# An encoder layer on one core: stores of a half on another queue, rows read in another order, and a rearranged opening

## The chip, the cores and the metric

The kernel runs on one core of a Trainium2 chip. TensorE multiplies (PE in the profile), VectorE (DVE), ScalarE (ACT) and GpSimd (POOL) do the rest, and SyncE (SP) issues most of the transfers. ScalarE and GpSimd have transfer queues of their own. The metric is the device time of the one launch in microseconds (us); lower is better. The inputs lie in the chip's main memory at the start, and both outputs have to be there at the end.

## The reference, cut to what matters

Two token sequences, `x_sample` (512 tokens) and `x_prompt` (1024 tokens), pass the same layer of width 1024 with the same weights:

```python
def trunk(x):                      # D_MODEL = 1024, D_FF = 4096, all in float32
    xn = rmsnorm(x, norm_mix_g)
    qa, ka, va, qb, kb, vb, ga, gb = split(xn @ w_in)
    o_a = grouped_query_attention(rope(rmsnorm(qa)), rope(rmsnorm(ka)), va)   # 8 heads of 64, 2 kv heads
    o_b = neighbourhood_attention(qb, kb, vb, b_rel_pos_bias)                 # 8 heads, 8x16 window
    merged = sigmoid(ga) * (o_a @ w_proj_a) + sigmoid(gb) * (o_b @ w_proj_b)
    x = x + merged @ w_out
    x = x + relu(rmsnorm(x, norm_mlp_g) @ w_mlp_up) ** 2 @ w_mlp_down
    return rmsnorm(x, norm_final_g)

def rmsnorm(x, g):
    return x * rsqrt(mean(x * x, -1) + 1e-6) * g
```

## The kernel before

**Tiles and products.** Tokens are handled in tiles of 128, in which a token is a partition and the 1024 features lie along the row. For a product the tile is transposed on TensorE (eight products of 128x128 with the identity). Every product is made three times to keep the accuracy of float32: an operand is split into a rounded upper part (names with `h` or `hi`, rounded by a copy on ScalarE) and what is left (`l` or `lo`, a subtraction on VectorE), and `mm3` (L203 to L205) multiplies hi by hi, hi by lo and lo by hi into one bank. So a weight block as it is loaded (`raw...`) passes ScalarE and VectorE before TensorE can use it.

**Stages.** `run` treats the sequences one after the other. The first trunk is `x_sample` (names with `0_` or rows 0 to 511), the second `x_prompt` (names with `1_` or rows 512 to 1535). In each it makes the normalised tiles and the products for q, k and v; then grouped-query attention, in which `ss` is a tile of scores, `ps` its exponentials (ScalarE), `pTs` the transposed exponentials in a bank, `pths` and `ptls` their split parts (ScalarE, VectorE) and `os` the output; then neighbourhood attention; then the output projections. The gate products (`gpss`, evicted by ScalarE into `sgs`) fill the attention's waits, and weights of the next step (`wghs`, `wgls`, `wh_vs`, `wl_vs`) are rounded meanwhile. After both trunks `mlp` makes the up and down products of both sequences together, by blocks.

**The opening.** Only the first trunk has it, as nothing covers its loads there. `ask_row` loads the weights of the first norm as one row (`grow`) and as a column form (`g8`), and sets a row of ones. `first_norm` sends six transposes of the identity into TensorE (`warm_up`), spreads the row over all 128 partitions by two products with `ones` (a product over one row; TensorE's records show each as two), and starts the norm of the first tile. `hi_of` and `lo_of` round the first weight blocks, `p0_first` transposes the first tile and splits it, `amid` is what it does between the two halves of that. `load_pad` and `setup_bias` (L168 to L177) load the relative position bias and write it back shifted into a buffer in main memory (`shifted`).

**The output stage of the second trunk.** `w_out` is applied in two halves of 512 columns (`for half in range(2)`), each over the eight token tiles `tt`. In the second half, for each tile: the old rows are read (`xr`), the product `op` is added, the sum is stored to `hd` (the residual, in main memory), squared on ScalarE and normalised, and the norm is stored to `hnd`. For the tiles 4 to 7 (`later`) the norm is made later, and `xr` has a slot of the tag `k4`, of which there are four, shared with the sums and norms of the tiles before. After tile 2 the norms are read back in pairs of tiles by `hn_raw` (rows `hn0_t`, j and j + 3, in slots of the tag `raw`, of which there are three), and after the tiles 3, 4 and 5 `pair_t` transposes a pair for the up product: `pt` at L331, pairs 0, 1 and 2, sixteen transposes each, the first eight from the tile j and the other eight from the tile j + 3.

**What sets the order.** A scheduler places the instructions of each engine by estimated costs; those under `tc.keep_in_program_order` stay as written in their engine's order. A change in one place can so rearrange others that no edited line names. Each queue of transfers issues in order: a load that waits for its slot holds those behind it.

## Time and profile before

| what | value |
|---|---|
| three runs | 2133.28, 2132.10, 2132.61 us |
| median | 2132.61 us |
| the profiled execution | 2133.53 us |
| its span, first to last instruction | 2131.8 us |
| granted TensorE clock, mean | 1.00 |
| TensorE, weight load | 2112.1 us (99%), 1848.0 us (87%) |
| VectorE, ScalarE, GpSimd | 1472.3 us (69%), 1116.1 us (52%), 390.7 us (18%) |
| moved | 264.85 MB read, 87.88 MB written, 165 GB/s |

The span is that of one profiled execution, 1.7 us shorter than the time of the same execution, which is 0.92 us above the median. A share is busy time over the span. In the rows of the timeline the first number is the start of the work in us from the span's start and the second its length; what stands in square brackets is the idle time of the engine just before and what ended it.

### The profile page before, as it was taken

The page shows a single profiled execution, that of the slowest core. Times are in us where ns is not written, and L with a number is a line of the kernel's source. Part 1 is how long each engine was busy: PE and PEld are TensorE (multiplying, and loading weights), DVE is VectorE, ACT ScalarE, POOL GpSimd, SP SyncE. Part 2 cuts the span into 40 slices and gives each one's busy share as a digit, 9 for nine tenths or more (in the row PEclk, how much of TensorE's full clock was granted, in tenths as well). Part 3 has the DMA queues.
Part 4 walks back from the last instruction along what each step waited for, and adds up shares of the span by engine and source line. Part 5 has one row for each costly group of instructions (what it writes and reads, how often), then busy time and mean ns, then how long its engine had stood idle before and what let it go on. Part 6 is the DMA issues. An engine that isn't in the chain of part 4 may idle for free.

```text
span 2131.8 us, 31800 instructions
## 1 busy us (share of the span) xinstructions
PE 2112.1 (99%) x10967; PEld 1848.0 (87%) x10967; DVE 1472.3 (69%) x2810; ACT 1116.1 (52%) x2351; POOL 390.7 (18%) x508
## 2 busy tenths in 40 slices
PE   9999999999999999999999999999999999999998
PEld 8887788988898888888888899999999988888887
DVE  6674686777667754657772877778777777659663
ACT  5664564566546644555431566566655643433352
POOL 3332420433233323433301200003000000000000
PEclk9999999999999999999999999999999999999999
DMA  6445567521221132433472666578444799688561
GB/s 188 136 124 147 155 192 244 187 72 35 58 86 54 40 112 84 126 101 110 145 244 101 206 200 193 161 248 210 158 145 158 259 356 336 214 269 286 177 198 69
DMA packets 319595, 350.92 MB, mean 165 GB/s; under 512 B 31168, under 2 KB 255048, under 8 KB 319433
## 3 DMA queue, kind: packets, MB, share of 16 engines
q1 hardware_dynamic: 278071, 279.91, 41.8%
q10 hardware_dynamic: 35682, 51.93, 7.0%
q0 software_dynamic: 5680, 17.04, 2.8%
q8 instruction: 87, 1.43, 0.3%
q14 instruction: 75, 0.61, 0.1%
HBM read 264.85 MB, written 87.88 MB: 165 GB/s over the span
## 4 chain that ended last, share of the span: by engine, by line
PE 82%; DVE 3%; DMA 2%; issue 2%; ACT 2%; POOL 1%; SPq 1%; ACTq 0%; POOLq 0%; DVEq 0%
PE dn L203 7%; PE dn L205 7%; PE dn L204 7%; PE pTs L827 3%; PE gpss L203 3%; PE gpss L205 3%; PE gpss L204 3%; PE uc L203 2%; PE uc L204 2%; PE ud L204 2%; PE ud L203 2%; PE ud L205 2%; PE uc L205 2%; PE ua L205 2%; PE ua L204 2%; PE ua L203 2%
## 5 line engine op out<-in xcount | busy, mean ns | idle before, releaser
L204 PE MATMUL dn<-wd,ah 128*128 128x512 f32 (+1 forms) x624 | 242.6, 389 | 0.0
L205 PE MATMUL dn<-wd,al 128*128 128x512 f32 (+1 forms) x624 | 242.6, 389 | 0.0
L203 PE MATMUL dn<-wd,ah 128*128 128x512 f32 (+1 forms) x624 | 242.6, 389 | 0.0
L1347 ACT ACTIVATE ah<-ar 128x512 fp32r<-128x512 f32 x168 | 104.2, 627 | 196.3 <-PE dn L204 172.8
L1348 DVE TENSOR_TENSOR al<-ar,ah 128x512 fp32r<-128x512 f32 x168 | 115.7, 696 | 73.2 <-ACT ah L1347 63.9
L205 PEld LDWEIGHTS dn<-wd,al 128*128 128x128 f32 x624 | 117.2, 188 | 24.3
L203 PEld LDWEIGHTS dn<-wd,ah 128*128 128x128 f32 x624 | 117.2, 188 | 24.0
L204 PEld LDWEIGHTS dn<-wd,ah 128*128 128x128 f32 x624 | 117.2, 188 | 24.0
L793 POOL TENSOR_SCALAR ps<-ps,rls 128x1024 f32<-128x1024 f32 (+1 forms) x96 | 96.8, 1010 | 215.7 <-DVE rls L792 205.1
L833 DVE TENSOR_TENSOR ptls<-pTs,pths 128x512 fp32r<-128x512 f32 x160 | 107.8, 687 | 39.2 <-ACT pths L832 38.6
L832 ACT ACTIVATE pths<-pTs 128x512 fp32r<-128x512 f32 x160 | 94.2, 598 | 74.1 <-PE pTs L827 71.4
L787 DVE TENSOR_REDUCE nms<-ss 128x1 f32<-128x1024 f32 (+1 forms) x96 | 99.7, 1041 | 22.3 <-PE ss L785 22.0
L188 POOL TENSOR_TENSOR rs_f<-ms_f,mhalf 128x1 f32<-128x1 f32 x6 | 4.0, 667 | 590.7 <-DVE ms_f L184 590.7
L203 PE MATMUL gpss<-xs_0h,w_gs 128*128 128x512 f32 x256 | 104.8, 409 | 1.5 <-DVE ptls L833 1.3
L790 ACT ACTIVATE ps<-ss,nms 128x1024 f32<-128x1024 f32 (+1 forms) x96 | 93.1, 971 | 23.1 <-DVE nms L787 20.6
L827 PEld LDWEIGHTS pTs<-ident,ps 128*128 128x128 f32 x640 | 78.1, 140 | 28.2 <-POOL ps L793 4.4
L204 PE MATMUL gpss<-xs_0l,w_gs 128*128 128x512 f32 x256 | 101.1, 395 | 0.0
L205 PE MATMUL gpss<-xs_0h,w_gs 128*128 128x512 f32 x256 | 101.0, 395 | 0.0
L827 PE MATMUL pTs<-ident,ps 128*128 128x128 f32 x640 | 98.9, 274 | 1.2 <-DVE ptls L833 0.3
L1347 ACT ACTIVATE A<-S 128x512 fp32r<-128x512 f32 x128 | 76.1, 624 | 31.9 <-DVE S L1410 26.7
L1348 DVE TENSOR_TENSOR A<-S,A 128x512 fp32r<-128x512 f32 x128 | 84.6, 686 | 4.3 <-ACT A L1347 4.3
L1466 ACT ACTIVATE c<-c 128x384 f32<-128x384 f32 x97 | 50.7, 524 | 69.3 <-DVE c L1465 69.2
(352 smaller groups left out, 6408.3 us busy)
## 6 DMA issues: line engine op xcount, KB each, us to landing
ar<-ud SPq DMA_DIRECT2D x120, 512.0 KB
br<-in_w_mlp_down_dram SPq DMA_DIRECT2D x72, 512.0 KB
rawu<-in_w_mlp_up_dram SPq DMA_DIRECT2D x64, 512.0 KB
ud<-c ACTq DMA_DIRECT2D x128, 192.0 KB
raw_gs<-in_w_in_dram SPq DMA_DIRECT2D x32, 512.0 KB
zgs<-sgs ACTq DMA_DIRECT2D x48, 256.0 KB
ud<-cs SPq DMA_DIRECT2D x64, 192.0 KB
raw_os<-in_w_out_dram SPq DMA_DIRECT2D x16, 512.0 KB
```

What stands on the lines that cost most here:

```text
L203: nc.tensor.matmul(out, ah, bh, start=start, stop=False, **kw)
L204: nc.tensor.matmul(out, ah, bl, start=False, stop=False, **kw)
L205: nc.tensor.matmul(out, al, bh, start=False, stop=stop, **kw)
L787: nc.vector.tensor_reduce(nm_, s, axis=AX.X, op=ALU.max, negate=True)
L790: nc.scalar.activation(p, s, AF.Exp, bias=nm_, accum_out=l)
L793: nc.gpsimd.tensor_scalar(p, p, rl, 1.0, op0=ALU.mult, op1=ALU.mult)
L827: nc.tensor.transpose(pt[:, j * P : (j + 1) * P], PP[u, j][:, kc * P : (kc + 1) * P], ident)
L832: nc.scalar.activation(hi, pt, AF.Copy)
L833: nc.vector.tensor_tensor(lo, pt, hi.bitcast(F32), op=ALU.subtract)
L1347: nc.scalar.activation(hi, src, AF.Copy)
L1348: nc.vector.tensor_tensor(lo, src, hi.bitcast(F32), op=ALU.subtract)
L1466: nc.scalar.activation(t, t, AF.Relu)
```

## The change

It has two groups of edits. In the opening, the norm weights are loaded into row 0 of a whole tile that is set to zero first, and the ones stand in row 0 of a tile of zeros, so that the spreading products contract over 128 rows in place of one; the warm-up has twelve transposes in place of six; and the rounding of the second weight block is cut in a lower and an upper half, of which the upper is rounded between the two halves of the first tile's split, with its subtraction on GpSimd. In the output stage of the second trunk, the sums of the second half's tiles 0 to 3 are stored by ScalarE's queue in place of SyncE's, and the rows `xr` of the tiles 5 to 7 are asked for between the reads of the norms.

```diff
--- before.py
+++ after.py
@@ -117,17 +117,19 @@
         )
 
     def ask_row(src, pool):
-        row = pool.tile([P, D], F32, tag="xn", name="grow", bufs=2)[0:1, :]
-        nc.scalar.dma_start(row, bass.AP(tensor=src.tensor, offset=src.offset, ap=[[0, 1], [1, D]]))
+        row = pool.tile([P, D], F32, tag="xn", name="grow", bufs=2)
+        tc.keep_in_program_order(nc.vector.memset(row, 0.0))
+        nc.scalar.dma_start(row[0:1, :], bass.AP(tensor=src.tensor, offset=src.offset, ap=[[0, 1], [1, D]]))
         g8 = sgp.tile([P, 512], F32, tag="sg", name="g8", bufs=2)[0:NC8, 0:P]
         nc.scalar.dma_start(g8, bass.AP(tensor=src.tensor, offset=src.offset, ap=[[P, NC8], [1, P]]))
-        ones = sgp.tile([P, 512], F32, tag="sg", name="ones", bufs=2)[0:1, 0:P]
-        tc.keep_in_program_order(nc.vector.memset(ones, 1.0))
+        ones = sgp.tile([P, 512], F32, tag="sg", name="ones", bufs=2)[:, 0:P]
+        tc.keep_in_program_order(nc.vector.memset(ones, 0.0))
+        tc.keep_in_program_order(nc.vector.memset(ones[0:1, :], 1.0))
         return row, g8, ones
 
     def first_norm(xt, gb, row, g8, ones, pool, nm):
 
-        warm_up(6)
+        warm_up(12)
         pt = big("grow")
         for q in range(2):
             qs = slice(q * 512, q * 512 + 512)
@@ -561,13 +563,15 @@
                         tc.keep_in_program_order(nc.sync.dma_start(x23[:, i, :], x[(2 + i) * P : (3 + i) * P, :]))
                         xt_of[2 + i] = x23[:, i, :]
 
-                    def hi_of(part, kb):
+                    lower, upper = slice(0, 2), slice(2, 4)
+
+                    def hi_of(part, kb, a=slice(0, 4)):
                         s_, cs = src[part, kb]
-                        tc.keep_in_program_order(nc.scalar.activation(wh[kb][:, :, cs], s_, AF.Copy))
-
-                    def lo_of(part, kb, eng=nc.vector):
+                        tc.keep_in_program_order(nc.scalar.activation(wh[kb][:, a, cs], s_[:, a], AF.Copy))
+
+                    def lo_of(part, kb, eng=nc.vector, parts=(lower, upper)):
                         s_, cs = src[part, kb]
-                        for a in (slice(0, 2), slice(2, 4)):
+                        for a in parts:
                             tc.keep_in_program_order(
                                 eng.tensor_tensor(
                                     wl[kb][:, a, cs], s_[:, a], wh[kb][:, a, cs].bitcast(F32), op=ALU.subtract
@@ -577,11 +581,13 @@
                     hi_of("q", 0)
                     xn, gcol = norm_rest()
                     lo_of("q", 0)
-                    hi_of("q", 1)
+                    hi_of("q", 1, lower)
                     st1 = []
 
                     def amid():
-                        lo_of("q", 1)
+                        hi_of("q", 1, upper)
+                        lo_of("q", 1, parts=(lower,))
+                        lo_of("q", 1, nc.gpsimd, (upper,))
                         st1.append(tr.stat(1, ph, x1, True))
 
                     tr.p0_first(xn, gcol, amid)
@@ -1160,13 +1166,24 @@
             def tmp_zs(name):
                 return ph.tile([P, 512], F32, tag="zs", name=name, bufs=6 if nxt is not None else 8)
 
-            def hn_raw(j):
+            def hn_raw(j, between=None):
                 res = []
                 for t in (j, j + 3):
                     r = rawp.tile([P, 1024], F32, tag="raw", name=f"hn0_{t}")
                     nc.sync.dma_start(r, hnd[t * P : (t + 1) * P, :])
                     res.append(r)
+                    if between:
+                        between.pop(0)()
                 return res
+
+            xr_of = {}
+
+            def rows_late(tt):
+                xr = ph.tile([P, D], F32, tag="k4", name=f"xr{N}_1_{tt}", bufs=4)[:, 0:512]
+                op = nc.sync.dma_start(xr, x[tt * P : (tt + 1) * P, 512:1024])
+                if tt == NT - 1:
+                    tc.keep_in_program_order(op)
+                xr_of[tt] = xr
 
             def pool_wp(shape, dt, name):
                 return ph.tile(shape, dt, tag="k4", name=name, bufs=4)
@@ -1232,10 +1249,12 @@
 
                     later = half == 1 and nxt is None and tb == 1
                     if later:
-                        xr = ph.tile([P, D], F32, tag="k4", name=f"xr{nm}", bufs=4)[:, 0:512]
+                        if tt not in xr_of:
+                            rows_late(tt)
+                        xr = xr_of.pop(tt)
                     else:
                         xr = tmp_zs(f"xr{nm}")
-                    nc.sync.dma_start(xr, x[tt * P : (tt + 1) * P, hc])
+                        nc.sync.dma_start(xr, x[tt * P : (tt + 1) * P, hc])
                     ht = hs_[tt // 2][:, tt % 2, :] if tb == 0 else None
                     if ht is None and half == 1 and not later:
                         ht = ph.tile([P, D], F32, tag="k4", name=f"ht{nm}", bufs=4)
@@ -1279,7 +1298,7 @@
                         if half == 1 and nxt is not None:
                             tc.keep_in_program_order(op)
                         if nxt is None:
-                            (nc.sync if half == 1 else nc.gpsimd).dma_start(hd[rows_, hc], ht[:, hc])
+                            (nc.scalar if half == 1 else nc.gpsimd).dma_start(hd[rows_, hc], ht[:, hc])
                         elif half == 1:
                             st = slice(0, D) if tb == 0 else hc
                             nc.gpsimd.dma_start(hd[rows_, st], ht[:, st])
@@ -1316,7 +1335,8 @@
                                 banks = [b_[:, q * 512 : q * 512 + 512] for b_ in both for q in range(2)]
                                 pair_t(f"0_{j}", j, hn_t, B0, banks, tmp_zs)
                                 if j < 2:
-                                    hn_t = hn_raw(j + 1)
+                                    early = [lambda: [rows_late(t) for t in (5, 6)], lambda: rows_late(7)]
+                                    hn_t = hn_raw(j + 1, early if j else None)
             while ahead:
                 nxt.p0_t(*ahead.pop(0))
```

The rows below are instructions in the order in which an engine has them, with the line, the operation and the program's names with a number for each tile; the line numbers of the kernel after are 2 to 20 higher.

SyncE's queue in the output stage of the second trunk, before; `hd` and `hnd` are the buffers in main memory, `hn0_t` the norms read back, `xrs1_1_t` the old rows of tile t:

```order
L1238 DMA xrs1_1_3_12766<-in_x_prompt_dram 128x512
L1282 DMA hd_86<-hs1_0_12388 128x512 x2
L1282 DMA hd_86<-hs1_1_12389 128x512 x2
L1167 DMA hn0_4_12864<-hnd_87 128x1024
L1238 DMA xrs1_1_4_12866<-in_x_prompt_dram 128x512
L1167 DMA hn0_2_12937<-hnd_87 128x1024
L1238 DMA xrs1_1_5_12941<-in_x_prompt_dram 128x512
L1238 DMA xrs1_1_6_13015<-in_x_prompt_dram 128x512
L1238 DMA xrs1_1_7_13044<-in_x_prompt_dram 128x512
L1167 DMA hn0_5_12939<-hnd_87 128x1024
```

The same place after:

```order
L1257 DMA xrs1_1_3_12775<-in_x_prompt_dram 128x512
L1173 DMA hn0_4_12873<-hnd_87 128x1024
L1183 DMA xrs1_1_4_12875<-in_x_prompt_dram 128x512
L1173 DMA hn0_2_12946<-hnd_87 128x1024
L1183 DMA xrs1_1_5_12948<-in_x_prompt_dram 128x512
L1183 DMA xrs1_1_6_12950<-in_x_prompt_dram 128x512
L1173 DMA hn0_5_12952<-hnd_87 128x1024
L1183 DMA xrs1_1_7_12954<-in_x_prompt_dram 128x512
```

The four stores to `hd` have left the queue, and the last read of a norm (`hn0_5`) stands ahead of the last old rows, not behind them. The stores are now on ScalarE, each ahead of the square of its tile. On TensorE pair 1 of the transposes stands six products later, pair 2 three.

TensorE in the first trunk's attention, before; `waits` is what an instruction waits for by semaphore:

```order
L785 MATMUL ss0_0_3_0_2_1103<-kTs0_0_215,qTs0_0_1_214 128x512
L804 MATMUL os0_0_1_0_1028<-ptls0_0_1_0_3_1037,vhls0_0_216 128x512
L827 MATMUL pTs0_0_2_0_2_1127<-ident_88,ps0_0_2_0_0_950 128x128 [waits Activation_49]
L827 MATMUL pTs0_0_2_0_2_1127<-ident_88,ps0_0_2_0_1_961 128x128
L827 MATMUL pTs0_0_2_0_2_1127<-ident_88,ps0_0_2_0_2_986 128x128
L827 MATMUL pTs0_0_2_0_2_1127<-ident_88,ps0_0_2_0_3_1019 128x128
L203 MATMUL gpss0_2304_3_0_1147<-xs0_0h0_158,w_gs0_2304_3_890 128x512 [waits DVE_49]
L204 MATMUL gpss0_2304_3_0_1147<-xs0_0l0_160,w_gs0_2304_3_890 128x512
L205 MATMUL gpss0_2304_3_0_1147<-xs0_0h0_158,w_gs0_2304_3_890 128x512
L784 MATMUL ss0_0_3_0_3_1136<-kTs0_0_215,qTs0_0_1_214 128x512 [waits Activation_49]
L785 MATMUL ss0_0_3_0_3_1136<-kTs0_0_215,qTs0_0_1_214 128x512
```

The same place after:

```order
L791 MATMUL ss0_0_3_0_2_1112<-kTs0_0_224,qTs0_0_1_223 128x512
L810 MATMUL os0_0_1_0_1037<-ptls0_0_1_0_3_1046,vhls0_0_225 128x512
L790 MATMUL ss0_0_3_0_3_1145<-kTs0_0_224,qTs0_0_1_223 128x512 [waits Activation_49]
L791 MATMUL ss0_0_3_0_3_1145<-kTs0_0_224,qTs0_0_1_223 128x512
L833 MATMUL pTs0_0_2_0_2_1136<-ident_88,ps0_0_2_0_0_959 128x128 [waits DVE_49]
L833 MATMUL pTs0_0_2_0_2_1136<-ident_88,ps0_0_2_0_1_970 128x128
L833 MATMUL pTs0_0_2_0_2_1136<-ident_88,ps0_0_2_0_2_995 128x128
L833 MATMUL pTs0_0_2_0_2_1136<-ident_88,ps0_0_2_0_3_1028 128x128
L205 MATMUL gpss0_2304_3_0_1156<-xs0_0h0_166,w_gs0_2304_3_899 128x512 [waits Activation_49]
```

The score tile `ss0_0_3_0_3` has moved ahead of the four transposes and of the gate product; the transposes now wait for VectorE, and the gate product for ScalarE.

ScalarE at the same place, before; `pths` are the upper parts of transposed exponentials, `sgs` the evicted gate product:

```order
L463 ACTIVATE sgs0_2304_2_0_1117<-gpss0_2304_2_0_891 128x512
L192 ACTIVATE wghs0_1_0_913<-rawkvs0_1_927 128x4x128
L192 ACTIVATE wghs0_1_1_917<-rawkvs0_1_927 128x4x128
L832 ACTIVATE pths0_0_2_0_0_1063<-pTs0_0_2_0_0_1058 128x512
L192 ACTIVATE wh_vs0_1_0_1048<-raw_vs0_1_0_1046 128x1024
L790 ACTIVATE ps0_0_3_0_1_1083,ls0_0_3_0_1_1084<-ss0_0_3_0_1_1078,nms0_0_3_0_1_1081 128x512
L192 ACTIVATE wh_vs0_1_0_1048<-raw_vs0_1_4_1053 128x1024
L832 ACTIVATE pths0_0_2_0_1_1099<-pTs0_0_2_0_1_1094 128x512
```

The same place after:

```order
L194 ACTIVATE wghs0_1_0_922<-rawkvs0_1_936 128x4x128
L194 ACTIVATE wghs0_1_1_926<-rawkvs0_1_936 128x4x128
L194 ACTIVATE wh_vs0_1_0_1057<-raw_vs0_1_0_1055 128x1024
L838 ACTIVATE pths0_0_2_0_0_1072<-pTs0_0_2_0_0_1067 128x512
L796 ACTIVATE ps0_0_3_0_1_1092,ls0_0_3_0_1_1093<-ss0_0_3_0_1_1087,nms0_0_3_0_1_1090 128x512
L194 ACTIVATE wh_vs0_1_0_1057<-raw_vs0_1_4_1062 128x1024
L838 ACTIVATE pths0_0_2_0_1_1108<-pTs0_0_2_0_1_1103 128x512
L465 ACTIVATE sgs0_2304_2_0_1126<-gpss0_2304_2_0_900 128x512
```

The eviction `sgs` has moved from the first place to the last, and the first `wh_vs` ahead of the first `pths`. On VectorE two subtractions of `wl_vs` now stand ahead of the `ptls` of the same transposes.

In the opening the order on ScalarE is: `g8`, then `grow` (before: the other way round), the square of the first tile, the first weight block, half of the second, the first four pieces of the tile's split, the other half, the square of the second tile, the other four pieces. VectorE starts with the zeros of the whole row tile and the two settings of `ones`. On SyncE the load of the bias (`pad`) now leads its part of the queue, ahead of the first values' weights (`raw_vs_0_0`), and the first store to `shifted` stands ahead of the second `raw_vs` and of three loads for the rotary tables.

## The prediction, as recorded before the changed kernel ran

> **What bounds the kernel now.** I read the page first, then the waits of TensorE, then the order of time around each place that the change touches.
>
> ```profile
> span 2131.8 us, 31800 instructions
> PE 2112.1 (99%) x10967; PEld 1848.0 (87%) x10967; DVE 1472.3 (69%) x2810; ACT 1116.1 (52%) x2351; POOL 390.7 (18%) x508
> ```
>
> TensorE is idle for 2131.8 - 2112.1 = 19.7 us in all, so removed waits can bring no more than that; beyond it only a faster TensorE clock can. The change adds six small transposes to TensorE and removes nothing, so its value is idle time moved about. Two of the longest single waits stand where the change acts:
>
> ```profile
> PE pt L331 <- DMA hn<-hnd: 1.5, 1, 1.5
> PE gpss L203 <- DVE ptls L833: 1.3, 1, 1.3
> ```
>
> Columns: who waits for whom, us in total, how often, the longest. The first is in the output projection of the second trunk, the second in the first trunk's attention, which no line of the diff names, but whose order the scheduler has rearranged.
>
> **Term 1: the late stores and reads (1150 to 1200 us).** SyncE's queue, the chain that ended last, TensorE, and the price of a store issued by ScalarE:
>
> ```profile
> 1151.56 16.65 SPq L1282 DMA_DIRECT2D hd<-hs  x4
> 1180.69 0.44 SPq L1167 DMA_DIRECT2D hn<-hnd  x1
> ...
> 1171.56 8.66 DMA hnd<-xnhs
> 1180.69 4.57 DMA hn<-hnd
> ...
> 1175.76 1.91 PE L331 MATMUL pt<-ident,hn 128*128 128x128 f32 x16
> 1182.07 0.39 PE L203 MATMUL ops<-wh_os,mgs 128*128 128x512 f32 x1
> 1182.30 0.39 PE L204 MATMUL ops<-wl_os,mgs 128*128 128x512 f32 x1
> 1182.81 1.06 PE L331 MATMUL pt<-ident,hn 128*128 128x128 f32 x8
> 1185.39 1.06 PE L331 MATMUL pt<-ident,hn 128*128 128x128 f32 x8 [1.52 <-DMA hn<-hnd]
> ...
> L1288 ACTq DMA_DIRECT2D hd<-xrs x4: 321/326/327, 1129.8 to 1146.1; - x4
> ```
>
> The last row read, hn5, was issued at 1180.69, because ahead of it on SyncE's in-order queue stood the last residual read (xr 7), whose slot came free when the store of 1171.56 had landed, 8.66 us later, at 1180.22. The read then took 4.57 us and TensorE stood 1.52 us. In the changed order hn5 stands ahead of xr 7. What holds it then is its own slot: that of hn1, free after the first eight transposes of pair 1. TensorE's order puts pair 1 six products later; one product takes 0.227 us (1182.07 to 1182.30), so pair 1 starts at 1175.76 + 1.36 = 1177.12. Sixteen transposes take some 1.8, so eight are done at 1178.0. Issue at 1178.1 and 4.57 us give a landing at 1182.7. Pair 2 starts three products later, at 1182.81 + 0.68 = 1183.5, and wants hn5 eight transposes on, at 1184.3: 1.6 us to spare, the wait goes. The start of pair 2 itself was 0.28 late (1182.30 to 1182.81 is 0.51, not 0.23); I count 0.08 of it. Gain 1.6 us. Bounds: 1.8 (both gaps gone); and if hn5 took 8.66 us it would land at 1186.8, 2.5 late, a loss of 1.0.
>
> The four stores moved from SyncE to ScalarE cost ScalarE 0.33 us each (L1288's row), and each stands ahead of the square of the same tile, so the norm and its store come 0.33 later; nothing waits for these within 1.6 us. What waits on ScalarE behind a store waits for the same VectorE sum that the square needs anyway. SyncE loses the four stores that held its queue from 1151.56 to 1168.2, so the two reads for pairs 1 and 2 leave about a microsecond sooner; no one waits for those.
>
> **Term 2: the rearranged attention (77 to 88 us).** ScalarE, VectorE and TensorE in order of time:
>
> ```profile
> 77.50 0.60 ACT L463 ACTIVATE sgs<-gpss 128x512 f32<-128x512 f32 x1
> 77.97 1.16 ACT L192 ACTIVATE wghs<-rawkvs 128x512 fp32r<-128x512 f32 x2
> 79.02 0.61 ACT L832 ACTIVATE pths<-pTs 128x512 fp32r<-128x512 f32 x1
> 79.49 1.08 ACT L192 ACTIVATE wh_vs<-raw_vs 128x1024 fp32r<-128x1024 f32 x1
> 80.44 0.71 ACT L790 ACTIVATE ps<-ss,nms 128x512 f32<-128x512 f32 x1
> ...
> 78.66 1.43 DVE L198 TENSOR_TENSOR wgls<-rawkvs,wghs 128x256 fp32r<-128x256 f32 x4 [0.16 <-ACT wghs L192]
> 80.00 0.68 DVE L833 TENSOR_TENSOR ptls<-pTs,pths 128x512 fp32r<-128x512 f32 x1
> 80.61 1.29 DVE L198 TENSOR_TENSOR wl_vs<-raw_vs,wh_vs 128x512 fp32r<-128x512 f32 x2
> ...
> 78.85 0.60 PE L827 MATMUL pTs<-ident,ps 128*128 128x128 f32 x4
> 80.74 0.50 PE L203 MATMUL gpss<-xs_0h,w_gs 128*128 128x512 f32 x1 [1.29 <-DVE ptls L833]
> ```
>
> Before, TensorE transposes at 78.85 into the bank that the gate's eviction (sgs, 77.50) had freed, then waits for ptls (80.00, done 80.68). In the new order the next score tile (ss 3_3) comes first, sgs has moved behind two weight roundings and two pths, and two wl_vs come ahead of ptls. By the rows: without sgs ScalarE runs 0.47 ahead; wghs 77.50, wh_vs 78.55, pths 79.50, the exponential 79.97, done 80.68. The score tile needs that exponential's bank, so TensorE stands from 78.85 to 80.7. VectorE: wgls until 79.7, wl_vs (1.2) until 80.9, ptls done at 81.6: the transposes, now in ptls' bank, start at 81.65 (two products end at 81.2: 0.45 idle) and end at 82.0. The next gate product now waits for sgs; ScalarE's second wh_vs (0.95) and pths (0.47) put it at 82.05 to 82.65, 0.7 idle more. Idle 1.85 + 0.45 + 0.7 = 3.0 against 80.74 - 79.2 = 1.5 before (four transposes issue in 0.35). The order behind it has more gate products in reserve, which I let win back 0.2. Loss 1.3 us. Bounds: 0 (an engine runs ahead of these rows) and 1.9 (nothing won back, and one more transpose waits 0.4 for VectorE). Other pieces reordered there had no wait over 0.3, and I give them nothing.
>
> **Term 3: the opening (0 to 18 us).**
>
> ```profile
> 0.73 0.53 ACTq L121 DMA_DIRECT2D grow<-in_norm_mix_g_dram  x1
> 0.90 0.17 DVE L125 MEMSET ones<- 1x128 f32 x1
> 13.28 1.27 DVE L394 SCALAR_TENSOR_TENSOR xns<-xts,rs_s,grow 128x1024 f32<-128x1024 f32 x1
> ...
> 1.35 1.54 PE L163 MATMUL warm<-ident 128*128 128x128 f32 x6 [1.35 <-POOL ident masks.py:199]
> 2.82 3.78 PE L134 MATMUL grow<-grow,ones 1*128 1x512 f32 x4
> 7.64 1.94 PE L410 MATMUL ptxs<-ident,xns 128*128 128x128 f32 x8 [1.03 <-DVE xns L152]
> 10.34 0.58 PE L205 MATMUL zs<-wghs,xs_0l 128*128 128x256 f32 x1 [0.34 <-DVE xs_0l L416]
> 13.07 0.41 PE L205 MATMUL zs<-wghs,xs_0l 128*128 128x256 f32 x1
> 13.60 0.28 PE L205 MATMUL zs<-wghs,xs_0l 128*128 128x256 f32 x1
> 14.94 1.07 PE L291 MATMUL ptxs<-ident,xns 128*128 128x128 f32 x8
> ...
> 8.76 1.14 ACT L413 ACTIVATE xs_0h<-ptxs,gcol 128x128 fp32r<-128x128 f32 x4 [0.20 <-PE ptxs L410]
> 10.81 1.16 ACT L413 ACTIVATE xs_0h<-ptxs,gcol 128x128 fp32r<-128x128 f32 x4
> 12.24 1.12 DVE L416 SCALAR_TENSOR_TENSOR xs_0l<-ptxs,gcol,xs_0h 128x128 fp32r<-128x128 f32 x4
> 12.41 0.56 POOL L188 TENSOR_TENSOR rs_s<-ms_s,mhalf 128x1 f32<-128x1 f32 x1 [5.20 <-DVE ms_s L184]
> ...
> 10.57 0.50 SPq L172 DMA_DIRECT2D pad<-in_b_rel_pos_bias_dram  x1
> 16.79 0.32 SPq L177 DMA_DIRECT2D shifted<-pad  x1
> ```
>
> TensorE's products last 0.41 until 13.07 and 0.28 from 13.60: until then it runs at about half speed, although it was busy without a break from 1.35 to 6.6 with six full transposes and four one-row products.
>
> The new 128x1024 memset starts where the memset of ones did, at 0.90. No row has its price; it lies between 0.17 (1x128) and 1.27 (the VectorE pass of its shape, L394), and I take 1.1, nearest the latter. The row's load waits for it, so it leaves at 2.0 instead of 0.73. It had landed by 2.82, so within 2.1; now by 4.1. Twelve transposes (1.54 for six) end at 4.3, so TensorE does not see that delay. The products end at 4.3 + 3.78 = 8.1 at the old speed, and the transposes of x, wanted at 7.64, would start 0.7 late; if the clock rises by about 6.9, not late.
>
> With the fast clock the first four transposes end 0.5 sooner (eight took 1.94 here, sixteen 1.91 in term 1), so ScalarE's first xs_0h starts at 8.27 instead of 8.76. The upper half of the second weight block, moved behind it, takes the 0.5 back: its second xs_0h stands at 10.82, was 10.81. VectorE gives up 0.6 of subtractions to GpSimd, which idled 5.2 us there, and can start its second xs_0l when the last xs_0h is done (10.81 + 1.16 = 11.97), at 12.02 instead of 12.24. xns and the transposes at 14.94 follow it: gain 0.2 us, and not the two microseconds that the clock would suggest, because VectorE and ScalarE end last there. Bounds: 0.5 gained (the first step's gain passes through whole); 1.0 lost (clock still slow: 0.7 late, and half a block of rounding now in the chain). I take 0.2 gained.
>
> The Trainium skill (TensorE: Matmul & The Clock Gate, Part 1) says that a free-running window of about 3.4 us of sustained matmul activity lifts the clock from half to full. By that alone the clock should have risen before 8.2 us in this trace, and it did not, so here the trace disagrees unless one-row products count for little. By the page term 3 is 0.2 gained to 0.5 lost, depending on where the window falls; if the row count is not what matters, it is the 1.0 lost.
>
> On SyncE pad's load now leads, and shifted, which waits for it, stands ahead of the second raw_vs and three rope loads: with the same 6.2 us (10.57 to 16.79) these leave some 4 us later. The wide slack ahead of their use, past 20 us, covers it; were it gone, ScalarE's rounding of raw_vs would be late next.
>
> **Sum.** 1.6 + 0.2 - 1.3 = 0.5 us gained. The profiled execution took 2133.53 with a span of 2131.8, so 2131.3 and 2133.0; the median of the runs, 0.92 below that execution, goes from 2132.61 to 2132.1. No difference under about 0.2% (4.3 us) can be told from none, and every bound above, even added up, stays inside it.
>
> **Rivals.**
> (a) The new attention order costs nothing: scheduled orders need not meet these rows again. 1.8 gained, 2130.8. For it: only one wait over 1 us stood there before. Against it: both new waits are on banks whose release I can place.
> (b) The other side: the row's load arrives after the twelve transposes, or the clock is late, and the products push the transposes of x. It decides from about 7.4 us as the end of the products: past it each microsecond costs one. Loss there 1.0, in all 1.6 - 1.0 - 1.3 = 0.7 lost, 2133.3. For it: 3.78 us of products now start 1.5 us later. Against it: twelve full transposes lead.
> (c) hn5 is not sooner on time, since the same bytes are in flight: term 1 is nothing, 1.1 lost, 2133.7.
> (d) The clock falls back in the 3 us of idleness at 79 to 83 us. Rising again took from 10.34 to 13.28 of products in the opening, about 3 us at half speed, 1.5 us lost: with the rest 1.0 lost, 2133.6. Against it: the 1.29 us gap here left products at 0.23 spacing. The same page of the Trainium skill says that an idle window of some 3.4 us halves the clock; the gaps here are broken by products, so it hardly applies.
>
> **Chances.** Forecast 0.48 (its own range 2131.1 to 2133.0), (a) 0.22, (b) 0.14, (c) 0.08, (d) 0.03; something unseen beyond 0.2%: 0.03 faster, 0.02 slower. Faster 0.03, same 0.95, slower 0.02. From (a) with both gains at their best (2130.0) to (c) with some noise (2134.2) leaves under 2 in 10 out.
>
> **What would show it.** Term 1: hn5 issued near 1178 and no wait before pair 2. Term 2: TensorE idle at about 79 to 83 for 3 us in three pieces, ended by an exponential, a ptls and an sgs. Term 3: matmuls at 0.28 before 9 us, second transposes of x near 14.7. The prediction is wrong if TensorE's sum of idle time moves by more than 4 us, or if a stretch outside these three does.

## The result and the profile after

The changed kernel takes 2137.26 us (median of 15 runs, 2135.42 to 2139.62) against 2132.61 (15 runs beside it, 2131.31 to 2135.11): 4.65 us slower, ratio 1.002 with a 95% interval of 1.0013 to 1.0027. Forecast were 2132.1 and a range up to 2134.2. Measured again later, the same pair gave 2137.97 against 2133.20 (ratio 1.0022, 1.0013 to 1.0031). Its profiled execution took 2138.04 us.

The head of the page of the changed kernel, and the longest waits of TensorE (who waits for whom, us in total, how often, the longest):

```profile
span 2136.3 us, 31820 instructions
PE 2114.0 (99%) x10973; PEld 1848.6 (87%) x10973; DVE 1472.0 (69%) x2811; ACT 1116.9 (52%) x2352; POOL 391.3 (18%) x509
...
PE grow L136 <- DMA grow<-in_norm_mix_g_dram: 3.1, 1, 3.1
PE obs L1070 <- DVE bhs L1048: 1.8, 3, 1.1
PE ss L790 <- ACT ps L796: 1.8, 1, 1.8
```

The wait for hn is gone from the list, as forecast. A wait of 3.1 us for the row of norm weights and one of 1.8 us in the attention are new, and the waits before obs (0.7 before) have grown. Where the time went is best read by comparing when the same product starts in both profiles. Groups of TensorE's products, with the first and the last start of a group, of the kernel before:

```profile
L203 PE MATMUL gpss<-xs_0h,w_gs x32: 387/390/502, 45.6 to 89.9; 128*128 128x512 f32 x32
L1007 PE MATMUL sbs<-kBs,qBs x192: 279/341/448, 181.1 to 1042.5; 128*128 128x384 f32 x128, 128*128 128x256 f32 x64
L203 PE MATMUL ops<-wh_os,mgs x192: 388/389/476, 329.4 to 1195.4; 128*128 128x512 f32 x192
```

and of the changed kernel:

```profile
L205 PE MATMUL gpss<-xs_0h,w_gs x32: 387/393/793, 48.5 to 97.2; 128*128 128x512 f32 x32
L1013 PE MATMUL sbs<-kBs,qBs x192: 278/341/449, 186.5 to 1049.1; 128*128 128x384 f32 x128, 128*128 128x256 f32 x64
L205 PE MATMUL ops<-wh_os,mgs x192: 388/389/477, 334.7 to 1200.3; 128*128 128x512 f32 x192
```

The first gate product is 2.9 us late (45.6 to 48.5): the opening. The first sbs is 5.4 late (181.1 to 186.5): the attention, which cost 2.8 by 110 us, less 0.3 won back behind it. The last sbs is 6.6 late (1042.5 to 1049.1), so a further piece was lost in the second trunk. The last ops is 4.9 late: the late stage gave 1.7 back against this profile of before. TensorE's idle time as a whole grew only from 19.7 to 22.3 us, since part of the loss is products that ran more slowly.

**The opening.** Issues of ScalarE's and SyncE's queue, and VectorE and TensorE, in order of time, changed kernel:

```profile
0.73 0.61 ACTq L124 DMA_DIRECT2D g<-in_norm_mix_g_dram  x1
2.04 0.23 ACTq L122 DMA_DIRECT2D grow<-in_norm_mix_g_dram  x1
...
0.73 0.38 SPq L262 DMA_DIRECT2D xts<-in_x_sample_dram  x1
1.17 0.97 SPq L541 DMA_DIRECT2D rawqs<-in_w_in_dram  x2
...
1.10 0.91 DVE L121 MEMSET grow<- 128x1024 f32 x1 [0.16 <-issue]
...
1.35 2.82 PE L165 MATMUL warm<-ident 128*128 128x128 f32 x12 [1.35 <-POOL ident masks.py:199]
7.27 3.56 PE L136 MATMUL grow<-grow,ones 128*128 128x512 f32 x4 [3.10 <-DMA grow<-in_norm_mix_g_dram]
10.91 1.09 PE L412 MATMUL ptxs<-ident,xns 128*128 128x128 f32 x8
```

Setting the tile to zero took 0.91 us, and the row left at 2.04 us, as forecast. But the products that need it began only at 7.27, 5.2 us later. Between 0.73 and 2.14 the loads of xts and of both rawqs, 512 KB each, were issued on SyncE's queue, ahead of these 4 KB; in the kernel before the row left beside the first of them. The trace also keeps the single packets that the transfer engines moved, and they show the row waiting behind these loads: its one packet of 4096 bytes began at 6.37 and took 0.16 us, when 870 of the 1024 packets of the two rawqs had started. The small load g, ahead of the row on ScalarE's queue, was done by 2.41, so it is not what held it. In the kernel before the row's packet began at 1.66.

**The attention.** TensorE in order of time, and the granted clock by stretch (columns: stretch, its length, busy time and count of PE, PEld, DVE, ACT, POOL, then PEclk, DMA share, GB/s):

```profile
81.53 0.40 PE L810 MATMUL os<-ptls,vhls 128*128 128x512 f32 x1
83.72 0.50 PE L790 MATMUL ss<-kTs,qTs 128*128 128x512 f32 x1 [1.79 <-ACT ps L796]
84.05 0.40 PE L791 MATMUL ss<-kTs,qTs 128*128 128x512 f32 x1
84.72 0.66 PE L833 MATMUL pTs<-ident,ps 128*128 128x128 f32 x4 [0.27 <-DVE ptls L839]
85.64 0.79 PE L205 MATMUL gpss<-xs_0h,w_gs 128*128 128x512 f32 x1 [0.26 <-ACT sgs L465]
86.22 0.63 PE L206 MATMUL gpss<-xs_0l,w_gs 128*128 128x512 f32 x1
...
85.50:86.00 0.50, 0.36 (x1) 0.37 (x2) 0.50 (x1) 0.50 (x2) 0.09 (x1) 0.59 1.11 334
86.00:88.00 2.00, 2.00 (x6) 1.52 (x6) 2.00 (x6) 1.44 (x4) 0.44 (x1) 0.50 0.99 286
88.90:89.10 0.20, 0.20 (x2) 0.18 (x1) 0.20 (x1) 0.00 (x0) 0.00 (x0) 0.74 0.99 238
```

The three pieces of idleness that the prediction named are there, ended by an exponential, a ptls and an sgs, in this order. Then products take 0.63 us, not 0.39: the granted clock is 0.50 from 85.59 (0.59 over the half microsecond means 0.09 at full speed) to 89.0, for 3.4 us. The Trainium skill (TensorE: Matmul & The Clock Gate, Part 1) gives such a window of about 3.4 us, free-running, and the trace agrees in length. The Trainium skill names an idle window, in the same part, as what halves the clock. Here the window ahead held products for 1.4 of its 3.4 us, and the clock fell all the same.

### The profile page after: what moved, and what is told of

It is laid out like the page before. It is cut to its first block, busy times and chain, and to the rows that moved or that the text cites. A ratio compares the mean times of both kernels' runs of the same rounds, so it can differ in the third digit from the quotient of the medians.

```text
span 2136.3 us, 31820 instructions
## 1 busy us (share of the span) xinstructions
PE 2114.0 (99%) x10973; PEld 1848.6 (87%) x10973; DVE 1472.0 (69%) x2811; ACT 1116.9 (52%) x2352; POOL 391.3 (18%) x509
## 4 chain that ended last, share of the span: by engine, by line
PE 82%; DVE 2%; ACT 1%; issue 1%; DMA 1%; POOL 1%; SPq 0%; ACTq 0%; POOLq 0%; DVEq 0%
PE dn L205 7%; PE dn L206 7%; PE dn L207 7%; PE pTs L833 3%; PE gpss L205 3%; PE gpss L207 3%; PE gpss L206 2%; PE uc L205 2%; PE ud L206 2%; PE uc L206 2%; PE ud L205 2%; PE uc L207 2%; PE ud L207 2%; PE ua L206 2%; PE ua L205 2%; PE ua L207 2%
## 5 line engine op out<-in xcount | busy, mean ns | idle before, releaser
L1367 ACT ACTIVATE ah<-ar 128x512 fp32r<-128x512 f32 x168 | 104.7, 628 | 207.7 <-PE dn L206 186.5
```

Source lines behind the costliest of these rows:

```text
L1367: nc.scalar.activation(hi, src, AF.Copy)
```

## The experiments

The runs were made on three chips, each beside the kernel before, whose median there was 2133.65, 2133.20 and 2133.91 us. The interval of each ratio is about 0.0009 to both sides, 1.9 us, so sizes below that rest on the profiles, and a profile is one execution. The two do not always agree: open_only has the highest median, but its profiled execution took 2136.77 us, less than that of after_again (2137.46). "Lost" and "won" below compare starts of the same products with those in the profile of before; two further profiles with the opening of before (late_only, before_again) run 0.2 us ahead of that one from the opening on, so 0.2 us is no difference there.

| run | median, us | median less that of before, us | ratio, 95% interval |
|---|---|---|---|
| late_only | 2132.97 | -0.7 | 0.9996 (0.9987 to 1.0005) |
| a_warm6 | 2135.27 | +1.6 | 1.0004 (0.9995 to 1.0013) |
| a_copy12 | 2135.37 | +1.7 | 1.0005 (0.9996 to 1.0014) |
| a_copy6 | 2132.78 | -0.9 | 0.9992 (0.9983 to 1.0001) |
| a_onerow | 2134.98 | +1.8 | 1.0007 (0.9998 to 1.0016) |
| open_only | 2138.54 | +5.3 | 1.0022 (1.0013 to 1.0031) |
| after_again | 2137.97 | +4.8 | 1.0022 (1.0013 to 1.0031) |
| best | 2132.21 | -1.7 | 0.9993 (0.9984 to 1.0002) |

The first four were run on the first of these chips, the next three on the second, best on the third. b_round and before_again are one profiled execution each (2132.64 and 2132.40 us).

**late_only**: the kernel before with the late edits of the change, and none of the opening's.

```
...
-                            (nc.sync if half == 1 else nc.gpsimd).dma_start(hd[rows_, hc], ht[:, hc])
+                            (nc.scalar if half == 1 else nc.gpsimd).dma_start(hd[rows_, hc], ht[:, hc])
...
-                                    hn_t = hn_raw(j + 1)
+                                    early = [lambda: [rows_late(t) for t in (5, 6)], lambda: rows_late(7)]
+                                    hn_t = hn_raw(j + 1, early if j else None)
```

> The kernel before with only the late part of the change (stores of the second half on ScalarE's queue, old rows of tiles 5 to 7 asked for between the reads of the norms). Theory of the three places (opening +2.9 us, attention at 79 to 92 us +2.8, late stage -1.7): the late gain stands by itself, so the median is 1.7 us under before, about 2130.9, TensorE has no wait for hn above 0.3 us between 1150 and 1200 us, and nothing differs ahead of 1150 us. Rival: the gain seen there is only the other side of the late opening (queues that had emptied), so the wait for hn stays near 1.5 us and the median within 0.5 us of before.

The profile has no wait of TensorE above 0.2 us between 1150 and 1200 us, and hn5 was issued at 1179.87, ahead of the last old rows. Against the profile of before that is 1.7 us won, as expected. The median says 0.7. Which of the two is right, before_again tells below. That nothing differs ahead of 1150 us did not hold: between 200 and 400 us this profile loses 1.7 us against that of before, although TensorE has the same order in both. Losses of a microsecond in one profile can come and go without any edit.

**a_warm6**: the changed kernel with before's warm-up.

```
-        warm_up(12)
+        warm_up(6)
```

> The changed kernel with six warm-up transposes as before, in place of twelve; everything else of the change stays. Its order in the attention is then that of before. Theory of the three places: the rearranged order in the attention is the cause of the loss there, so the stretch 77 to 92 us costs what it cost before (one wait of about 1.3 us, clock 1.00 throughout) and the median falls by about 2.8 us against the changed kernel, to about 2134.5; the wait for the row of norm weights in the opening grows by the six transposes' 1.4 us, to about 4.5 us. Rival: the clock fell because the opening ran late and shifted the attention against the clock's windows, not because of the order; then a half-clock piece of about 3.4 us stays near 80 us and the median falls by under 1.2 us.

```profile
PE grow L136 <- DMA grow<-in_norm_mix_g_dram: 4.1, 1, 4.1
...
PE gpss L205 <- DVE ptls L839: 1.3, 1, 1.3
```

The wait for the row is 4.1 us and the attention has its old wait of 1.3 us and nothing more: between 70 and 110 us no product loses anything against before (3.4 us late ahead of it and 3.5 behind). So six small transposes at 3 us, which only shift the scheduler's estimates, are what rearranged the attention at 80 us. The rival is out.

**a_copy12**: the row is loaded at once into a tile that is free until later, and copied.

```
+        row1 = gb[0:1, :]
-        nc.scalar.dma_start(row[0:1, :], ...)
+        nc.scalar.dma_start(row1, ...)
...
+        tc.keep_in_program_order(nc.vector.tensor_scalar(row[0:1, :], row1, 1.0, None, op0=ALU.mult))
```

> The changed kernel, but the row of norm weights is loaded at once into the tile gb, which is free until later, and copied from there by VectorE into row 0 of the zeroed tile; all other engines keep the order of the changed kernel. Theory of the three places: the opening's loss is the row's load, which the setting to zero pushed behind the 512 KB loads; loaded at 0.7 us it lands by 2.9, the copy of one row (about 1 us, from 0.91 for setting the whole tile) ends by 4.1, the products start behind the twelve transposes near 4.2 us, and TensorE does not wait for the row; the first transposes of x start no later than 8 us, and the median is 2.9 us under the changed kernel or lower, 2134.4 or less. Rival: the products over 128 rows and the order of the rounding are what costs; then the opening stays late by more than 1.5 us against before and the median within 1 us of 2137.3.

```profile
2.40 0.68 DVE L129 TENSOR_SCALAR grow<-gbs 1x1024 f32<-1x1024 f32 x1
...
3.97 3.60 PE L138 MATMUL grow<-grow,ones 128*128 128x512 f32 x4
7.66 1.09 PE L414 MATMUL ptxs<-ident,xns 128*128 128x128 f32 x8
```

Issued at 0.73, the row was there by 2.40, within 1.7 us, and the products followed the transposes without a wait. The opening's loss is 0.1 us where it was 2.9, with the products over 128 rows and the rounding order still in: the rival is out. That the 512 KB loads are what holds a row issued later is read from the packets above; moving those loads was not tried. The attention lost 2.6 us again, with a half-clock piece from 82.5.

**a_copy6**: the same with six warm-up transposes.

> The row loaded at once and copied, as in the run beside it, and six warm-up transposes, so that the attention has the order of before. Theory of the three places: both losses are gone and the late gain is left, so 2137.3 - 2.9 - 2.8 = 2131.6 at most, and 2130.9 (before less 1.7) if the opening costs what it did before: 1 to 1.7 us under before. The products wait about 1 us for the copy between the warm-up and about 4 us. Rival: a further cost of the change lies elsewhere (a wait of 1.5 us for a weight load near 1015 us stood in the changed kernel's profile too); then it stays at 2132.6 or above.

Both losses are gone: level with before at 60 us, 0.4 late at 110, and 0.9 under before by the median, a little less than the 1 to 1.7 expected. The wait near 1015 us, the rival's further cost, is gone as well, so it comes with the twelve transposes. The clock was up at 4.9 us, and the opening gained nothing by it.

**a_onerow**: the changed kernel with before's spreading of the norm weights (one row, not zeroed) and twelve transposes.

```
-        row = pool.tile([P, D], F32, tag="xn", name="grow", bufs=2)
-        tc.keep_in_program_order(nc.vector.memset(row, 0.0))
-        nc.scalar.dma_start(row[0:1, :], ...)
+        row = pool.tile([P, D], F32, tag="xn", name="grow", bufs=2)[0:1, :]
+        nc.scalar.dma_start(row, ...)
...
-        ones = sgp.tile([P, 512], ...)[:, 0:P]
...
+        ones = sgp.tile([P, 512], ...)[0:1, 0:P]
...
```

> The changed kernel with the spreading of the norm weights as before (one row, loaded at once, products over one row), with its twelve warm-up transposes, its rounding order and its late part. TensorE, SyncE and GpSimd have exactly the changed kernel's order. Theory of the three places: without the zeroed tile there is no wait for the row, and the opening is 0.3 to 1.0 us over before (products end near 8.0, x's transposes wait for them); the clock rises only after a window of whole products, between 10 and 13.5 us, because one-row products do not count as activity. In the attention the order of the changed kernel costs 1.0 us of idle time, and 1.7 us more when the clock's window of 3.41 us holds nearly all of that idle time. Median about 1.4 us over before (0.3 + 2.8 - 1.7), down to 0 if the clock falls in few executions. Rival: one-row products count, so the clock rises by 8.2 us and the first transposes of x take about 1.1 us, not 1.9.

```profile
4.10 3.78 PE L134 MATMUL grow<-grow,ones 1*128 1x512 f32 x4
7.82 1.97 PE L410 MATMUL ptxs<-ident,xns 128*128 128x128 f32 x8
13.07 0.39 PE L204 MATMUL zs<-wgls,xs_0h 128*128 128x256 f32 x1
13.43 0.29 PE L203 MATMUL zs<-wghs,xs_0h 128*128 128x256 f32 x1
```

TensorE was never idle from 1.35 to 9.9 us here, and yet its products were slow until 13.3. With products over 128 rows (a_copy6, a_copy12, best) it was up at 4.9, 7.4 and 8.4. So one-row products did not count for the clock. That it was the transposes which did not count is ruled out by open_only: there twelve of them, from 1.35 to 4.17 us, were all that TensorE did, and the clock was up at 4.64. The opening lost 0.3 us, the attention 2.2.

**open_only**: the change without its late edits.

```
...
-                            (nc.scalar if half == 1 else nc.gpsimd).dma_start(hd[rows_, hc], ht[:, hc])
+                            (nc.sync if half == 1 else nc.gpsimd).dma_start(hd[rows_, hc], ht[:, hc])
...
-                                    early = [lambda: [rows_late(t) for t in (5, 6)], lambda: rows_late(7)]
-                                    hn_t = hn_raw(j + 1, early if j else None)
+                                    hn_t = hn_raw(j + 1)
```

> The change without its late part: stores of the second half on SyncE's queue and old rows as before. Theory of the three places: 2.9 + 2.8 us over before, 5.7, and 1.2 to 1.7 us over the changed kernel beside it; the wait for hn is back near 1185 us with about 1.5 us. Rival: the late part gains nothing of its own, and the median equals that of the changed kernel within 0.5 us.

The median is 0.6 us above the changed kernel, less than the 1.2 to 1.7 expected. And the wait for hn, which this kernel should have had, was not in its profile: pair 2 ran its sixteen transposes in one piece. Its opening lost only 1.7 us, not 2.9: the clock, up at 4.64, stayed up until 8.05, so that the products with the late row took 2.42 us in place of 3.56.

**after_again**: the changed kernel once more.

> The changed kernel once more, beside the two others and with a new profile. Theory of the three places: 4 to 5 us over before; the wait for the row near 3.1 us and no wait for hn; the three waits at 80 to 86 us add up to about 2.3 us again. If the clock falls there depends on where the window's border lies: it stays at 1.00 if the border splits the longest wait, and the stretch then costs 1.0 us and not 2.8. Rival: the half-clock piece belongs to the order alone and is there in each profile at the same distance behind the wait.

```profile
PE grow L136 <- DMA grow<-in_norm_mix_g_dram: 2.6, 1, 2.6
...
83.96 0.50 PE L790 MATMUL ss<-kTs,qTs 128*128 128x512 f32 x1 [1.79 <-ACT ps L796]
84.96 0.66 PE L833 MATMUL pTs<-ident,ps 128*128 128x128 f32 x4 [0.27 <-DVE ptls L839]
85.88 0.50 PE L205 MATMUL gpss<-xs_0h,w_gs 128*128 128x512 f32 x1 [0.27 <-ACT sgs L465]
86.22 0.40 PE L206 MATMUL gpss<-xs_0l,w_gs 128*128 128x512 f32 x1
...
84.00:86.00 2.00, 1.47 (x7) 0.80 (x8) 2.00 (x5) 2.00 (x4) 0.69 (x1) 1.00 0.74 216
86.00:88.00 2.00, 2.00 (x8) 1.41 (x9) 2.00 (x5) 1.69 (x4) 0.19 (x1) 1.00 0.95 256
```

The same three waits, and the clock stays at 1.00: products take 0.40 behind them. Counted from the moment at which the clock had risen (11.84), in steps of 3.41 us, a border fell at 83.5 and split the idle time into 1.3 and 1.0 us; in the first profile the window from 82.2 to 85.6 held 2.0 of it. The fall thus depends on where the window lies, not on the order alone. The stretch cost 1.9 us here, and 2.2, 2.2, 2.6 and 2.8 in the four profiles of this order in which the clock fell: the fall adds 0.3 to 0.9 us, not half of 3.4. Why so little was not tried; a slower TensorE probably meets fewer waits behind the stretch. The 1.0 us that I expected without the fall was too little.

**b_round**: the kernel before with only the rounding order changed, one profiled execution.

```
...
-                    hi_of("q", 1)
+                    hi_of("q", 1, lower)
...
                     def amid():
-                        lo_of("q", 1)
+                        hi_of("q", 1, upper)
+                        lo_of("q", 1, parts=(lower,))
+                        lo_of("q", 1, nc.gpsimd, (upper,))
```

> The kernel before with only the order of the rounding changed (upper half of the second weight block later, its subtraction on GpSimd). One look at the opening. By the step of the prediction the second xs_0l of the first tile starts at 12.0 and the second tile's transposes 0.2 us sooner than before's 14.94. By the profile of the run with copied row and six warm-ups it starts 0.25 us later (second xs_0h at 11.3, not 10.8, since the rounding of the upper half stands ahead of the second tile's square on ScalarE), and the transposes come no sooner than before.

```profile
9.79 0.65 ACT L568 ACTIVATE wghs<-rawqs 128x512 fp32r<-128x512 f32 x1
11.34 1.16 ACT L413 ACTIVATE xs_0h<-ptxs,gcol 128x128 fp32r<-128x128 f32 x4
...
12.54 1.13 DVE L416 SCALAR_TENSOR_TENSOR xs_0l<-ptxs,gcol,xs_0h 128x128 fp32r<-128x128 f32 x4
15.00 1.07 PE L291 MATMUL ptxs<-ident,xns 128*128 128x128 f32 x8
```

The second xs_0l starts at 12.54, 0.3 later than before's 12.24; the second tile's transposes are 0.06 later. The upper half now stands ahead of the second tile's square, and here it costs ScalarE 0.5 us that nothing gives back. This does not yet test the prediction, whose step had the fast clock bring that 0.5 in, and the clock of b_round rose only at 12.7. The run with the fast clock in time and this rounding order is a_copy6, ScalarE:

```profile
8.20 0.63 ACT L572 ACTIVATE wghs<-rawqs 128x512 fp32r<-128x512 f32 x1 [0.96 <-DMA rawqs<-in_w_in_dram]
8.73 1.13 ACT L417 ACTIVATE xs_0h<-ptxs,gcol 128x128 fp32r<-128x128 f32 x4
...
11.29 1.15 ACT L417 ACTIVATE xs_0h<-ptxs,gcol 128x128 fp32r<-128x128 f32 x4
```

There the first xs_0h starts at 8.73, not at the 8.27 of the prediction, because ScalarE waited until 8.20 for the load of the second weight block; the second is at 11.29, not 10.82.

**best**: a_copy6 with the edit of b_round taken back. **before_again**: the kernel before, no edit, one more profiled execution.

> The kernel before with the row of norm weights loaded at once and copied into a zeroed tile (products over 128 rows), six warm-up transposes, the order of the rounding as before, and the late part of the change. The attention keeps the order of before. Theory, after eight runs: the late part is worth 0.6 us on the median (late_only 0.7 under before, after_again 0.6 under open_only), since the wait for hn that it removes was 1.5, 0.6 and 0 us in three executions that lack it; the early clock is worth 0.3 to 0.5 us if the order of the rounding is left as before (in the run with it the second xs_0h stood at 11.3, not 10.8). Together 0.9 to 1.2 us under before. Rival: VectorE and ScalarE bound the opening whatever the clock, so only the 0.6 us are left, and the second tile's transposes start at 14.9 as before.

> The kernel before, unchanged: one more look, to see how its waits differ between executions. Theory: the wait for hn near 1185 us is not 1.5 us again but anything from 0 to 1.5, as in the two other kernels with the late stage of before (0.6 and 0 us); the wait of 1.3 us at 79 us in the attention comes back with the same length, as it did in four profiles with that order; no wait for raw_pas near 1010 us, which only the five kernels with twelve warm-up transposes showed. Rival: the wait for hn is fixed by the order, 1.5 us in each execution of this kernel.

The second tile's transposes in best and in before_again, and the transposes of pair 2 in before_again:

```profile
14.56 1.06 PE L295 MATMUL ptxs<-ident,xns 128*128 128x128 f32 x8
...
14.70 1.07 PE L291 MATMUL ptxs<-ident,xns 128*128 128x128 f32 x8
```

```profile
1183.35 2.09 PE L331 MATMUL pt<-ident,hn 128*128 128x128 f32 x16
```

In before_again pair 2 runs in one piece: the wait of 1.5 us on which term 1 rested is not there in another execution of the same kernel. Four profiles of the old late stage (before, b_round, open_only, before_again) show 1.5, 0.6, 0 and 0 us. The order of the queue is the same each time: in before_again the last old rows ahead of hn5, which wait for their slot, left at 1179.34 and not 1180.27, and hn5 at 1179.76 and not 1180.69, although TensorE was 0.5 us later. Its wait of 1.3 us in the attention came back and no wait for raw_pas was there, both as expected. best starts the second transposes at 14.56, 0.4 us sooner than before's 14.94 but only 0.1 sooner than before_again's 14.70, so what the earlier clock is worth with the rounding left alone is not shown. Its median is 1.7 us under before, more than the 0.9 to 1.2 expected, with an interval that still reaches 1.0002. It is the lowest of all kernels run, not proven faster than before, and clearly faster than the change.

## Why the prediction was wrong, point by point

**Term 3, the opening (0.2 gained forecast; 2.9 and 3.1 lost in two profiles of the changed kernel).** The step that failed is the landing of the row: "it had landed by 2.82, so within 2.1; now by 4.1". I moved the issue by 1.3 us and kept the flight time of the old place, while in just that time 1.5 MB of other loads are issued. From issue to use it took 5.2 us, not 2.1. a_copy12 shows the cause: with the early issue back the loss is 0.1. Rival (b) had the mechanism, a row later than the twelve transposes, but was priced at 1.0 and 0.14 of chance; by its own point of 7.4 us, the measured end of the products (7.27 + 3.56 = 10.83) gives 3.4. The step of the rounding was wrong as well, by 0.5: with the fast clock ScalarE's first xs_0h was to start at 8.27 and started at 8.73 (a_copy6), since the load of the second weight block, not TensorE, came last. That VectorE and ScalarE end last whatever the clock was right in a_copy6.

**Term 2, the attention (1.3 lost forecast; 1.9 without and up to 2.8 with the fall of the clock).** The mechanism was right: from the rows above the gaps beyond normal spacing are 2.19 - 0.23, 0.67 - 0.23 and 0.92 - 0.35, together 2.97, where 3.0 was forecast. Mis-sized were the 0.2 that the order behind would win back (it won nothing and waited 0.3 to 0.4 more), which gives the upper bound of 1.9, and rival (d), given 0.03: the clock fell in four of five profiles of this order, and cost 0.3 to 0.9 us where (d) had 1.5. "[T]he gaps here are broken by products, so it hardly applies" was the failed step.

**Term 1, the late stage (1.6 gained forecast; 0.6 and 0.7 by the medians of two pairs, neither clear of noise).** The path was right. SyncE's queue, changed kernel:

```profile
1184.77 0.33 SPq L1173 DMA_DIRECT2D hn<-hnd  x1
1185.38 0.33 SPq L1183 DMA_DIRECT2D xrs<-in_x_prompt_dram  x1
```

hn5 left ahead of xr 7, at 1178.2 if the 6.6 us of lateness are taken off (forecast 1178.1), and the wait was in none of eight profiles with the late edits. But the wait was 1.5 us only in the one execution that I had. Half the term was the luck of a profile.

**Not foreseen: a load in the second trunk.** In all five profiles with twelve transposes ScalarE waits for the load of raw_pas near 1012 us, and TensorE then for bhs, which costs 1.0 to 1.5 us; in none of the seven others does it. ScalarE, changed kernel and before:

```profile
1009.40 1.15 ACT L194 ACTIVATE w_pas<-raw_pas 128x512 fp32r<-128x512 f32 x2
1014.59 0.63 ACT L194 ACTIVATE w_pas<-raw_pas 128x512 fp32r<-128x512 f32 x1 [2.19 <-DMA raw_pas<-in_w_proj_a_dram]
```

```profile
1004.36 1.15 ACT L192 ACTIVATE w_pas<-raw_pas 128x512 fp32r<-128x512 f32 x2
1007.27 0.63 ACT L192 ACTIVATE w_pas<-raw_pas 128x512 fp32r<-128x512 f32 x1
```

The orders around it are the same, and the load was issued 0.1 us behind the w_pas at 1009.40 and 1004.36 in both, but it took 5.1 us in place of less than 2.9. The packets of the trace show what held it. In each of the five, 480 of the load's 512 packets had ended 2.6 us after the issue; the other 32, one sixteenth, were held back, and packets on SyncE's queue ran again just as a 16 KB packet of the instruction queue (by that name, a piece of the program itself) had ended, 2.8 to 3.3 us after the issue. The last of the load's packets then came more than a microsecond late. In the seven others such a packet, of about 1 us, ran at nearly the same moment, and all 512 packets of the load had ended by 2.6 us. So a fetch of instructions on the same one of the 16 transfer engines is the likely holder; that it is the same engine is inferred, as the packets do not name theirs. Why six instructions added early bring the two together is open. Between 110 and 150 us each of the five lost 0.4 us, and between 150 and 250 us each won 1.1 to 1.2 against before's profile, of which four of the others won 0.3 to 0.5 too; I did not follow it. These are stretches outside the three of the prediction, which it had named as a sign of being wrong.

**The sum.** For the first profile, in lateness of the same products: 2.88 (opening) + 2.82 (attention) - 0.66 (from 110 to 1000 us) + 1.54 (near 1012) - 1.72 (late stage) - 0.36 (behind 1200) = 4.5, which is the difference of the two spans (2136.3 - 2131.8). In the prediction's range the low end was mis-added: term 1 at 1.8, term 3 at 0.5 and no loss in the attention give 2130.3, not 2130.0; it changes nothing here.

## What to carry to other kernels

Price a delayed load by what is in flight when it leaves, not by its old flight time: 4 KB issued 1.3 us later came 4 us later and more. Before a wait from one profile is booked as a gain, read it in a second execution. And a few instructions added where the engine is idle can rearrange scheduled work far behind them: here that cost more than the edit itself could have brought, and leaving the six transposes away removed it.

## What the runs showed of the hardware

The one-row products did not count for TensorE's clock: in the kernel before, the window from 3.20 to 6.61 (counted back in steps of 3.41 us from the rise at 13.44) held nothing else and no idle time, and the products stayed slow until 13.4; a_onerow shows the same. (Ahead of its first rise the trace records no clock, so the speed there is read from how long products take.) A window with twelve transposes and 0.6 us of idle time lifted it (open_only, 1.23 to 4.64). Once it had risen, its changes within an execution lay whole numbers of 3.41 us apart (10.50 and 85.59 in the changed kernel: 22 windows), while the place of the first differs between executions. Over all twelve profiles, after the first rise, each window with 1.79 us or more of idle TensorE in it was followed by half the clock (the smallest: 1.79, 1.80, 1.92, 2.02, 2.06), and each with 1.54 or less was not. No window lay between 1.54 and 1.79. So a window need not be idle throughout to halve the clock. So the same waits cost 0.3 to 0.9 us more in one execution than in the next. A wait of 1.3 us, as in the attention of before, was safe; 2.3 us of waits within 4 us were safe only in the execution in which a border of the windows split them.
